# The input norm's weights as a column at the eviction of transposed chunks, dummy transposes ahead, and first gates in chains of 512 tokens

## The chip, the cores and the metric

The kernel runs on one core of one Trainium2 chip. Its time is in device microseconds (us), the median of several executions. Everything below names the core's engines as the profile does: PE (TensorE, matrix products; PEld is its weight loads), DVE (VectorE), ACT (ScalarE), POOL (GpSimd) and SP (SyncE, which here only issues transfers). SBUF is the on-chip memory, PSUM the eight banks of 128 x 512 floats into which PE writes.

## The reference

One layer of an encoder over 16 meta tokens and 1024 tokens of width 1024. The part that matters here is its beginning:

```python
def rms_norm(x, g):
    y = x * lax.rsqrt(jnp.mean(x * x, axis=-1, keepdims=True) + EPS)
    return y * g

a = rms_norm(h, norm_mix)                       # h: 16 meta tokens, then 1024 tokens
(q_na, k_na, v_na, q_hg, z_f, z_b, i_hg, g_hg, gate_na, gate_hg) = split_cols(a @ w_in)
log_f = logaddexp(log(lb), log1p(-lb) + log_sigmoid(z))      # per direction, from z_f and z_b
k = -expm1(log_f)                               # that is (1 - lb) * sigmoid(-z)
```

Here lb comes from a softmax over two rows of logits (`hg_lb_logits`). The rest of the layer (neighbourhood attention, a bidirectional gated recurrence over four heads, output projections, a feed-forward block, the final norm) follows and is not touched by the change.

## The kernel before

**Numbers and layout.** A product in full precision is made of three matmuls (`mm3`, lines 121 to 124): both operands are split into a rounded part `hi` and a remainder `lo`, and hi\*hi, hi\*lo and lo\*hi are accumulated in one PSUM bank. All projections contract over the 1024 features, in `KC` = 8 pieces of 128 (an index k), so one product of up to 512 tokens is 24 matmuls. The normed input must therefore lie with features on partitions: the tiles `aT[h]` hold it as hi and lo, `[128, 8, 512]` for each half h of 512 tokens, and the 16 meta tokens stand behind the first half, at columns 512 to 527.

**The beginning, function `start()`.** Tokens come as eight tiles `xt[i]` of 128 tokens x 1024 features, and the meta tokens as `xm` of 16 x 1024 (tile 8). For each tile:

- `square(i)`: ACT squares the tile with a running sum (line 554); POOL then works out 1/sqrt(mean + eps) in two operations on one column (lines 92 and 93);
- `scale(i)`: DVE multiplies the tile by that column and by the norm's weights in one scalar_tensor_tensor (line 559). The weights are needed along the free axis on all partitions, so a row of 1024 weights is spread over the partitions first, by two products with a column of ones (line 542) and two copies by ACT (line 545);
- `transpose(i)`: eight transposes on PE into two banks, each bank holding four feature pieces of 128 tokens (line 567);
- `evict(i)`: ACT copies a bank as hi, DVE takes the remainder as lo (lines 575 and 576).

Between the tiles stand the splits of the first two weight blocks (`load_block`, lines 112 and 113: hi by ACT, lo by DVE) and parts of the first products. `first_products` (a generator, one step per k) makes the gates' projections of head 0: forward (d = 0) and backward (d = 1), each for the two halves of the tokens. The forward one for the first half is made in two pieces, the first 256 tokens early, then 256 tokens and the 16 meta tokens in one piece of 272 columns. `start()` makes the first piece and the backward product of the first half; `rest()` makes the others. At the end of `start()` comes the small softmax for lb (tiles `lt`, `mx`; lines 631 to 642). The meta tokens are the last tile.

**The gates.** `gates_of` takes the finished products in the order in which they stand in `firsts`. For each, ACT makes two Sigmoids from PSUM (lines 220 and 221) and DVE three tensor_scalar operations (lines 222 and 225); for the meta tokens the same on 16 columns (lines 229 to 232). Its tiles (`T0`, `X0`, `Y`, ...) come from the pool `hp`, which is opened after `start()` has closed its own pool.

**What sets the order.** `start()`, `rest()` and the first part of head 0 stand in a block whose order is written out by hand: every engine issues its instructions in the order of the program's text. What follows the block is ordered by a planner that works with estimated times. SP issues the loads of tiles and weights, in the order x0, x1, forward weights, x2, x3, x4, backward weights, x5, x6, x7; ACT issues the weights of the norm, the meta tokens, the logits `lt` and a gain. Weight blocks pass through two `raw` buffers (line 102), so the third block's load waits until the first is split. PSUM at this stage: two banks for `mm`, two for `mx`, four for `a`.

## Time and profile before

| | |
|---|---|
| time, median of 3 runs | 1534.61 us (1534.53 to 1535.69) |
| the profiled execution: span | 1534.6 us |
| PE busy | 1503.2 us (98%) |
| DVE, ACT, POOL busy | 1031.3, 658.9, 380.1 us |
| granted TensorE clock, mean | 0.999 |
| HBM read, written | 139.56 MB, 54.53 MB |

The page of a profile gives the busy time of each engine, the span in 40 slices, the transfers by queue, the chain of work that ended last, and the costliest groups of instructions. A group's row reads: line, engine, operation, what is written from what, shapes, count | busy us, mean ns of one | idle time of the engine ahead of them and what ended it. A row of the timeline reads: start, duration (of several merged instructions with their count x2, x8: of all of them), engine, line, operation, and in brackets the idle time of the engine ahead of it. A row of the windows reads: the stretch, its length, the busy time of PE, PEld, DVE, ACT and POOL with counts, then the granted clock, the share of the DMA engines and GB/s. A row of the transfers ends in the KB of one and the us from its issue to its landing.

### The profile page before, as it was taken

The numbers are of one execution on the slowest core, as the hardware profiler recorded it, in microseconds if no ns is written. First come the engines' busy times: TensorE is split into PE (matmuls) and PEld (weight loads), VectorE is DVE, ScalarE is ACT, GpSimd is POOL, SyncE is SP. The second block draws the span as 40 slices with busy tenths as digits, with TensorE's granted clock in tenths as the row PEclk, the third lists the DMA queues.
The fourth block names the chain that finished last, engine by engine and source line by source line (L and its number), as shares of the span: only waits on it lengthen the run. The fifth ranks groups of instructions, "written<-read, shape, count | busy, mean of one in ns | idle before, by whom it ended". The sixth has DMA issues, their size and how long they took to land.

```text
span 1534.6 us, 23451 instructions
## 1 busy us (share of the span) xinstructions
PE 1503.2 (98%) x9192; PEld 1252.2 (82%) x9192; DVE 1031.3 (67%) x1603; ACT 658.9 (43%) x1175; POOL 380.1 (25%) x354
## 2 busy tenths in 40 slices
PE   7999999999999998999999999999999999999998
PEld 5888888878888887888888887888888888888886
DVE  6676666654876877666476358877777544877876
ACT  6231313125665666434123135555555533434444
POOL 2323131316315400011000122533333300231142
PEclk9999999999999999999999999999999999999999
DMA  4111111114123128434746123444444676563224
GB/s 167 45 29 56 29 56 29 56 29 130 56 66 120 62 65 272 138 124 153 261 163 233 42 97 117 165 154 153 153 153 150 208 266 236 193 232 111 96 83 151
DMA packets 142449, 195.61 MB, mean 127 GB/s; under 512 B 8049, under 2 KB 90097, under 8 KB 142338
## 3 DMA queue, kind: packets, MB, share of 16 engines
q1 hardware_dynamic: 133216, 172.53, 33.9%
q10 hardware_dynamic: 6946, 14.24, 2.4%
q0 software_dynamic: 2176, 7.34, 1.3%
q8 instruction: 72, 1.18, 0.3%
q14 instruction: 39, 0.32, 0.1%
HBM read 139.56 MB, written 54.53 MB: 126 GB/s over the span
## 4 chain that ended last, share of the span: by engine, by line
PE 89%; DVE 5%; issue 2%; ACT 2%; DMA 1%; POOL 1%; ACTq 0%; POOLq 0%; SPq 0%; DVEq 0%
PE mm L122 11%; PE mm L123 11%; PE mm L124 11%; PE mm L1349 5%; PE pa L1349 4%; PE pb L856 4%; PE pb L858 4%; PE pb L857 4%; PE pc L1349 4%; PE pb L1349 4%; PE pc L858 3%; PE pc L857 3%; PE pc L856 3%; PE pa L858 2%; PE pa L857 2%
## 5 line engine op out<-in xcount | busy, mean ns | idle before, releaser
L122 PE MATMUL mm<-aT,hi 128*128 128x512 f32 (+2 forms) x640 | 229.8, 359 | 2.4 <-DVE QX L727 1.5
L124 PE MATMUL mm<-aT,lo 128*128 128x512 f32 (+2 forms) x640 | 226.9, 354 | 0.5 <-DVE lo L113 0.5
L123 PE MATMUL mm<-aT,hi 128*128 128x512 f32 (+2 forms) x640 | 225.8, 353 | 0.0
L122 PEld LDWEIGHTS mm<-aT,hi 128*128 128x128 f32 x640 | 121.4, 190 | 16.6 <-issue 1.7
L124 PEld LDWEIGHTS mm<-aT,lo 128*128 128x128 f32 x640 | 121.3, 190 | 14.2 <-DVE lo L113 1.0
L123 PEld LDWEIGHTS mm<-aT,hi 128*128 128x128 f32 x640 | 121.4, 190 | 12.5
L97 DVE TENSOR_TENSOR dl<-ur,dh 128x1024 fp32r<-128x1024 f32 x54 | 71.0, 1315 | 87.3 <-ACT dh L96 87.1
L96 ACT CAST dh<-ur 128x1024 fp32r<-128x1024 f32 x54 | 56.9, 1054 | 166.5 <-issue 91.1
L112 ACT CAST hi<-raw 128x1024 fp32r<-128x1024 f32 x36 | 37.8, 1050 | 96.7 <-PE mm L123 68.4
L1154 DVE TENSOR_TENSOR wl<-raw,wh 128x512 fp32r<-128x512 f32 x50 | 40.9, 822 | 36.5 <-ACT wh L1153 36.3
L1158 ACT ACTIVATE uv<-uv 128x512 f32<-128x512 f32 x48 | 30.4, 633 | 80.0 <-DVE uv L1266 48.9
L1154 DVE TENSOR_TENSOR wl<-sx,wh 128x512 fp32r<-128x512 f32 x70 | 61.0, 882 | 3.4 <-ACT wh L1153 3.3
L1153 ACT CAST wh<-sx 128x512 fp32r<-128x512 f32 x70 | 42.3, 620 | 42.3 <-PE pc L857 24.0
L1439 POOL TENSOR_TENSOR w<-w,tt 128x512 f32<-128x512 f32 x16 | 23.4, 1460 | 132.9 <-DVE tt L1438 113.2
L300 POOL TENSOR_TENSOR Y<-X,TN 128x512 f32<-128x512 f32 x20 | 34.3, 1713 | 84.5 <-DVE X L297 84.5
L113 DVE TENSOR_TENSOR lo<-raw,hi 128x1024 fp32r<-128x1024 f32 x36 | 46.8, 1300 | 9.8 <-ACT hi L112 9.7
L782 DVE CUSTOM_DVE_ANT_0 pr<-nsc,NB 128x432 f32<-128x432 f32 (+1 forms) x64 | 35.2, 560 | 26.7 <-PE nsc L777 26.5
L409 DVE TENSOR_TENSOR QQ<-QQ,TN 128x512 f32<-128x512 f32 x48 | 35.1, 742 | 22.9 <-PE sc L404 22.9
L856 PE MATMUL pb<-nt,wh 128*128 128x512 f32 x128 | 50.2, 392 | 0.3 <-DVE uv L1236 0.2
L122 PE MATMUL mm<-wh,mT 128*128 128x512 f32 x128 | 50.1, 392 | 0.0
L858 PE MATMUL pb<-nt,wl 128*128 128x512 f32 x128 | 49.8, 389 | 0.0
L124 PE MATMUL mm<-wh,mT 128*128 128x512 f32 x128 | 49.8, 389 | 0.0
(391 smaller groups left out, 4370.9 us busy)
## 6 DMA issues: line engine op xcount, KB each, us to landing
raw<-in_w_in SPq DMA_DIRECT2D x56, 512.0 KB, 4.0
ur<-usp SPq DMA_DIRECT2D x54, 512.0 KB, 3.4
raw<-in_w_up SPq DMA_DIRECT2D x16, 1024.0 KB, 6.1
usp<-us SPq DMA_DIRECT2D x60, 256.0 KB, 2.2
sg<-gsp SPq DMA_DIRECT2D x16, 512.0 KB, 3.3
w<-in_w_dn SPq DMA_DIRECT2D x16, 512.0 KB, 4.5
usp<-uv SPq DMA_DIRECT2D x30, 256.0 KB, 3.2
gsp<-gv ACTq DMA_DIRECT2D x24, 256.0 KB, 2.4
```

The source lines that it names most:

```text
L96: act.copy(hi, src)
L97: dve.tensor_tensor(lo, src, hi.bitcast(F32), op=ALU.subtract)
L113: dve.tensor_tensor(lo[:, :kc], raw[:, :kc], hi[:, :kc].bitcast(F32), op=ALU.subtract)
L122: pe.matmul(ps, lh, rh, start=first, stop=False)
L123: pe.matmul(ps, lh, rl, start=False, stop=False)
L124: pe.matmul(ps, ll, rh, start=False, stop=last)
L856: pe.matmul(ps, lhs[0][:, c], rhs[0][:, k], start=first and k == 0, stop=False, skip_group_check=True)
L857: pe.matmul(ps, lhs[0][:, c], rhs[1][:, k], start=False, stop=False, skip_group_check=True)
L858: pe.matmul(ps, lhs[1][:, c], rhs[0][:, k], start=False, stop=k == 3, skip_group_check=True)
L1153: act.copy(v(hi), src)
L1154: dve.tensor_tensor(v(lo), src, v(hi).bitcast(F32), op=ALU.subtract)
L1349: pe.matmul(ps, a[n == 2][:, q, j * P:(j + 1) * P], b[n == 1][:, q], start=first and n == 0, stop=last and n == 2, skip_group_check=True)
```

## The change

The norm's weights no longer multiply the tiles ahead of the transposes. They come as a tile `g_col` of 128 x 8, feature on partition (the host passes the vector reshaped), and multiply when a transposed bank is evicted, since there the features lie on partitions. The banks hold now one feature piece k of all 512 tokens of a half (`turn`, `chunk`), and one eviction makes hi by an ACT multiply and lo by a DVE scalar_tensor_tensor. Tiles are scaled in place by their column alone. The meta tokens come first, with the softmax's first steps; they take their weights in one DVE product over 16 columns a piece.

PE gets transposes of the identity into a bank that nobody reads (`keep_warm`): 20 at the start, 8 after the meta tokens and 5 after each of tiles 0 to 2. Transposes of pieces 0 to 5 of the first half follow tile by tile; pieces 6 and 7 and the second half go piece by piece.

The forward product of the first half is one chain over 512 tokens, and the 16 meta tokens are a product of their own. The first gate is taken within `start()`, ahead of the scales of tiles 6 and 7. For this the gates' tiles come from a pool `hq` that is opened ahead of `start()`.

Work moves between engines: the split of the forward weights takes half of its lo to POOL, and the backward weights are split by POOL alone; the squares of tiles 6 and 7 go from ACT to DVE. Loads go in the order x0 to x3, forward weights, backward weights, x4 to x7; ACT's queue starts with the meta tokens, then `g_col`.

```diff
-                ev(ps[:, :n], t0, n)
+                if n:
+                    ev(ps[:, :n], t0, n)
...
+    def first_products(d, h, tag, n=TH):
+
+        nm = NM if n == NM else 0
+        c0 = TH if nm else 0
+        ps = bank(tag, "mm").rearrange("p a b -> p (a b)")[:, :n]
...
+        act.dma_start(xt[8], meta)
+        act.dma_start(g_col, g_mix)
...
+        for i in range(4):
             load_x(i)
+        raws = [load_raw(w_in[:, c:c + P], KC) for c in (C_ZF, C_ZB)]
+        for i in range(4, 8):
             load_x(i)
...
+            if eng is act:
+                act.activation(junk[:n], t, AF.Square, accum_out=sums[i][:n])
+            else:
+                dve.tensor_tensor_reduce(out=junk[:n], in0=t, in1=t, scale=1.0, scalar=0.0,
+                                         op0=ALU.mult, op1=ALU.add, accum_out=sums[i][:n])
...
         def scale(i):
+            dve.tensor_scalar(xt[i], xt[i], rs[i][:xt[i].shape[0]], None, op0=ALU.mult)
...
+        def keep_warm(n):
+            for j in range(n):
+                pe.transpose(warm[:, j % 4], ident, ident)
+
+        def turn(i, ks):
+            for k in ks:
+                pe.transpose(pts[i // 4, k][:, i % 4], xt[i][:, k * P:(k + 1) * P], ident)
+
+        def chunk(h, k):
+            pts[h, k] = bank("a", "pt")
+            for i in range(4 * h, 4 * h + 4):
+                turn(i, (k,))
+
+        def evict(h, k):
+            hi, lo = (t[:, k, :TH] for t in aT[h])
+            pt = pts[h, k].rearrange("p a b -> p (a b)")
+            act.mul(hi, pt, g_col[:, k:k + 1])
+            dve.scalar_tensor_tensor(lo, pt, g_col[:, k:k + 1], hi.bitcast(F32), op0=ALU.mult, op1=ALU.subtract)
...
+        def block(d):
+            hi, lo = blocks[d] = [wp.tile([P, KC, P], F32R, tag=t, name=t) for t in ("hi", "lo")]
+            copy, first = (pool.tensor_copy, pool) if d else (act.copy, dve)
+            copy(hi, raws[d])
+            for e, c in (first, slice(0, 4)), (pool, slice(4, 8)):
+                e.tensor_tensor(lo[:, c], raws[d][:, c], hi[:, c].bitcast(F32), op=ALU.subtract)
+
+        keep_warm(20)
         square(8)
+        root(8)
         scale(8)
+        ptm = bank("mm", "ptm")[:, 0].rearrange("p (k t) -> p k t", t=NM)
+        for k in range(KC):
+            pe.transpose(ptm[:, k], xt[8][:, k * P:(k + 1) * P], ident[:NM, :NM])
+        keep_warm(8)
         dve.tensor_tensor(mx, lt[:, :, 0], lt[:, :, 1], op=ALU.max)
+        for q in range(2):
+            pool.tensor_tensor(lt[:, :, q], lt[:, :, q], mx, op=ALU.subtract)
+        for k in range(6):
+            pts[0, k] = bank("a" if k < 4 else "mx", "pt")
+        for i in range(4):
+            square(i)
+            root(i)
+            scale(i)
+            turn(i, range(6))
+            if i < 3:
+                keep_warm(5)
+            if i == 0:
+                mh, ml = (t[:, :, TH:TH + NM] for t in aT[0])
+                dve.tensor_tensor(am, ptm, fap(g_col, 0, [[1, KC], [0, NM]]), op=ALU.mult)
+                act.copy(mh, am)
+                dve.tensor_tensor(ml, am, mh.bitcast(F32), op=ALU.subtract)
+                act.activation(lt.rearrange("p a b c -> p (a b c)"), lt.rearrange("p a b c -> p (a b c)"), AF.Exp)
+            if i == 1:
+                pool.tensor_tensor(mx, lt[:, :, 0], lt[:, :, 1], op=ALU.add)
+            if i == 2:
+                dve.reciprocal(mx, mx)
+        block(0)
...
+        f0 = first_products(0, 0, "mm")
+        evict(0, 0)
+        evict(0, 1)
+        for k in range(6):
+            some(f0, 1)
+            if k < 2:
+                chunk(0, k + 6)
+            evict(0, k + 2)
+            if k == 2:
+                square(4)
+        block(1)
+        some(f0, 2)
+        square(5)
+        root(4)
+        root(5)
+        for i in (6, 7):
+            square(i, dve)
+            root(i)
+        scale(4)
+        scale(5)
+        b0 = first_products(1, 0, "mm")
+        next(gates)
+        scale(6)
+        scale(7)
+        some(b0, 6)
+        f1 = first_products(0, 1, "mx")
+        for k in range(KC):
+            chunk(1, k)
+            evict(1, k)
+            if k < 2:
+                some(b0, 1)
+            if k > 2:
+                some(f1, 1)
         p0s.close()
+        return f1
+
+    def rest(gates, f1):
+
+        list(f1)
         next(gates)
         next(gates)
+        list(first_products(0, 0, "mm", NM))
+        next(gates)
+        early[C_Q] = block_of(C_Q)
+        list(first_products(1, 1, "mx"))
+        next(gates)
...
+        hq = hps.enter_context(tc.tile_pool(name="hq", bufs=1, reuse_waits="tile"))
...
+        f1 = start(ahead[0])
+        hp = hps.enter_context(tc.tile_pool(name="hp", bufs=1, reuse_waits="tile"))
+        rest(ahead[0], f1)
```

## The prediction

> **What bounds the kernel now.** I read the page first, then the early stretches window by window, then the first 60 us as a timeline by engine, then the groups with shapes kept apart for the price of each new operation.

> ```profile
> span 1534.6 us, 23451 instructions
> ...
> PE 1503.2 (98%) x9192; PEld 1252.2 (82%) x9192; DVE 1031.3 (67%) x1603; ACT 658.9 (43%) x1175; POOL 380.1 (25%) x354
> ```

> ```profile
> 0.00:10.00 10.00, 4.42 (x7) 1.83 (x8) 1.29 (x2) 5.21 (x8) 2.65 (x12) 1.00 0.85 290
> 10.00:20.00 10.00, 7.80 (x37) 7.03 (x36) 9.67 (x11) 7.87 (x15) 4.52 (x7) 1.00 0.81 295
> 20.00:30.00 10.00, 9.03 (x55) 7.35 (x54) 7.18 (x10) 7.34 (x14) 2.57 (x8) 1.00 0.18 52
> 30.00:40.00 10.00, 10.00 (x55) 7.99 (x53) 7.33 (x17) 5.54 (x12) 1.46 (x6) 1.00 0.01 2
> ```

> The first number after the stretch is its length, then the busy time of PE, PE's weight loads, DVE, ACT and POOL. PE idles 31.4 us in all, and 8.75 of them lie in the first 30 us, the part that the change rewrites; from 30 us on PE is full. So whatever the rewritten part gains or loses moves the rest as a whole, and it is enough to predict when the last of the first products ends. Before, that is where the next projection's first matmul starts, 48.70:

> ```profile
> 9.33 3.97 PE L567 MATMUL pt<-ident,na 128*128 128x128 f32 x16 [2.27 <-DVE na L559]
> ...
> 19.76 1.91 PE L567 MATMUL pt<-ident,na 128*128 128x128 f32 x8
> ...
> 22.95 1.04 PE L567 MATMUL pt<-ident,na 128*128 128x128 f32 x8
> ...
> 34.06 0.66 PE L567 MATMUL pt<-ident,na 16*128 16x16 f32 x8
> ```

> ```profile
> 40.23 0.28 PE L122 MATMUL mm<-aT,hi 128*128 128x272 f32 x1
> ...
> 43.23 0.39 PE L122 MATMUL mm<-aT,hi 128*128 128x512 f32 x1
> ...
> 48.70 0.39 PE L122 MATMUL mm<-aT,hi 128*128 128x512 f32 x1
> ```

> Prices on PE: 24 matmuls of 512 columns take 43.23 to 48.70, 5.47 us (0.68 per k of three); 24 of 272 columns take 3.00 (0.125 each). Eight transposes take 1.91 at 19.76 but 1.04 at 22.95: PE runs at about half pace until some 21 us, although the granted clock reads 1.00. Warm, a transpose is 0.13.

> **The change, part by part.** (1) *The matmul count.* The first forward product ran as 256 and 272 columns, at most 3.00 each when warm; now it runs as 512 (5.47) and 16. The 16-column matmul with a full weight load is not in the trace. Its bounds are 0.075 (the 16x16 transposes, 8 in 0.66 with their tail) and 0.125 (272 columns): 1.8 to 3.0 for 24. I take 2.4, between them, as the load of full weights is common to it and the 272-column row. Together 7.9, at least 1.9 more than 6.0; against that, part of the 256 columns ran ahead of the rise in pace.

> (2) *The dummy transposes* are 43 in all, 20 before anything else. The first 20 cost at most 20 x 0.24 = 4.8 us from 1.5 us on, ahead of any data. Those between the tiles stand in waits for DVE: zero, as long as the scale of the next tile ends later than they do.

> (3) *The start of the chain.* Meta tokens and the lower-bound softmax come first now, and they stand ahead of tile 0 on three engines: on DVE the max over lt, on POOL the two subtractions ahead of tile 0's root, on ACT the meta copy and the Exp ahead of tile 1's square.

> ```profile
> xt<-in_x SPq DMA_DIRECT2D x8, 512.0 KB, 7.2
> ...
> xm<-in_meta ACTq DMA_DIRECT2D x1, 64.0 KB, 4.7
> ...
> lt<-in_lbl ACTq DMA_DIRECT2D x1, 8.0 KB, 7.0
> ```

> ```profile
> 1.65 0.43 ACTq L529 DMA_DIRECT2D lt<-in_lbl  x1
> ...
> 2.10 3.07 SPq L522 DMA_DIRECT2D xt<-in_x  x3
> ...
> 5.87 1.06 ACT L554 ACTIVATE na<-xt 128x1024 f32<-128x1024 f32 x1
> ...
> 7.10 0.58 ACT L545 COPY g_bc<-pg 128x512 f32<-128x512 f32 x1
> 7.11 0.19 POOL L92 TENSOR_SCALAR rtm<-ssq 128x1 f32<-128x1 f32 x1 [5.68 <-ACT na L554]
> ...
> 7.99 1.28 DVE L559 SCALAR_TENSOR_TENSOR na<-xt,rs,g_bc 128x1024 f32<-128x1024 f32 x1 [7.99 <-POOL rs L93]
> ...
> 33.82 0.15 DVE L631 TENSOR_TENSOR mx<-lt 128x8 f32<-128x8 f32 x1
> ...
> 34.05 0.20 POOL L632 TENSOR_TENSOR lt<-lt,mx 128x8 f32<-128x8 f32 x1 [3.52 <-DVE mx L631]
> ```

> On SP's queue tiles 2 and 3 now go ahead of both weight blocks: fourth, as at 2.10 before, tile 3 lands near 2.10 + 7.2 = 9.3, ahead of its square. The weights, fifth and sixth now, are wanted only from 15.5 on, and tiles 4 to 7 after 24; the next weight block's load, which waits for a raw buffer, is wanted after 46. No load sets the path. lt lands at 1.65 + 7.0 = 8.65. It stays third on ACT's queue, so I keep 8.65; bounds 6.0 (where xm landed) and 10.0. Then max 0.2, two subtractions 0.4, root to scale 0.88 (7.11 to 7.99): tile 0's scale starts at about 10.2, where it was 7.99. The Exp on 16 columns, the meta product on DVE and its copy on ACT then add about 0.85 (four times the Exp's 0.21) before tile 1's square, which starts near 11.8.

> ```profile
> 34.44 0.21 ACT L637 ACTIVATE lt<-lt 128x16 f32<-128x16 f32 x1 [1.04 <-POOL lt L633]
> ```

> (4) *The scale.* It loses its tensor operand (the weights), so it becomes a one-source operation. The nearest row is L786, in place with one column scalar.

> ```profile
> L786 DVE TENSOR_SCALAR pr<-pr,rc x64: 360/437/1057, 381.8 to 577.1; 128x432 f32<-128x432 f32 x48, 128x288 f32<-128x288 f32 x16
> ```

> From 288 columns (0.36) to 432 (0.437) is 0.53 ns a column, so 1024 cost 0.75 against 1.28. [...] If a scale cost 1.08 (one column per 1.04 ns), the sum below would be 1.3 worse.

> Squares on ACT follow each other every 1.23 (5.87, then the next operation at 7.10). Tile 3's square ends at 11.8 + 3 x 1.23 = 15.5; root to scale 0.88, and 0.3 for one root waiting behind a scale, so its scale runs 16.7 to 17.45.

> (5) *The weights at the eviction.* ACT's copy from PSUM becomes a multiply with a column; the nearest row is the copy that it replaces, 0.59, less than DVE's part and so hidden behind it. DVE's lo becomes a SCALAR_TENSOR_TENSOR from PSUM:

> ```profile
> L575 ACT CAST aT<-pt 128x512 fp32r<-128x512 f32 x16 | 8.9, 588 | 6.1 <-PE pt L567 6.1
> ```

> ```profile
> L782 DVE CUSTOM_DVE_ANT_0 pr<-nsc,NB 128x432 f32<-128x432 f32 x48 | 28.4, 596 | 0.0
> ...
> L492 DVE SCALAR_TENSOR_TENSOR ot<-opt,gain_sb,gs 128x512 f32<-128x512 f32 x8 | 5.7, 748 | 6.1 <-PE opt L490 6.1
> ...
> L97 DVE TENSOR_TENSOR lo<-raw,hi 128x512 fp32r<-128x512 f32 x8 | 5.5, 683 | 0.0
> ...
> L782 DVE DVE_READ_ACCUMULATOR2_ANT mn<- 128x1 f32 x64 | 5.3, 83 | 0.0
> ```

> ```profile
> 15.23 1.28 DVE L576 TENSOR_TENSOR aT<-pt,aT 128x512 fp32r<-128x512 f32 x2
> ...
> 18.82 1.27 DVE L559 SCALAR_TENSOR_TENSOR na<-xt,rs,g_bc 128x1024 f32<-128x1024 f32 x1
> ```

> In a row such operations overlap by 0.08 (two of 0.68 in 1.28), so 0.67 each, 5.4 for eight. DVE first does its half of the forward weight block (0.68), and it can meet POOL there:

> ```profile
> 16.01 0.19 POOL L92 TENSOR_SCALAR rtm<-ssq 128x1 f32<-128x1 f32 x1 [0.28 <-ACT na L554]
> ...
> 19.16 0.99 POOL L92 TENSOR_SCALAR rtm<-ssq 128x1 f32<-128x1 f32 x1 [2.33 <-ACT na L554]
> ...
> 46.45 1.30 POOL L286 TENSOR_TENSOR kd<-X,Y 128x512 f32<-128x512 f32 x1
> 50.72 2.23 POOL L286 TENSOR_TENSOR kd<-X,Y 128x512 f32<-128x512 f32 x1 [2.96 <-DVE X L225]
> ```

> The 0.19 operation at 19.16 takes 0.99, to 20.15, until DVE's ends at 20.09; the second kd takes 2.23 for the first one's 1.30. So POOL and a DVE operation with two SBUF inputs shut each other out. [...] I charge half of one POOL operation, 0.65 (bounds 0 and 1.3). The last lo of the first half then ends at 17.45 + 0.68 + 0.65 + 5.4 = 24.2.

> (6) *Tiles 4 to 7.* DVE now squares tiles 6 and 7. L782 is the nearest reduce: 432 columns in 0.596, so 1024 in 1.21 at 1.04 ns a column, plus 0.08 to read the sum: 2.6 for two. Then four scales at 0.67, and in the middle the first gate:

> ```profile
> 41.06 0.55 DVE L222 TENSOR_SCALAR T<-sf,oml_sb,lb_sb 128x512 f32<-128x512 f32 x1 [2.48 <-ACT sf L220]
> ...
> 41.82 0.35 DVE L225 TENSOR_SCALAR Y<-sn,oml_sb 128x256 f32<-128x256 f32 x1
> ```

> 1.1 us. The Sigmoids ahead of it and their table load on ACT are hidden: ACT ends its last square near 24, and DVE reaches the gate at about 28.7. With 0.5 for the roots behind POOL's second block (bounds 0 and 2.4), tile 7's scale ends at 24.2 + 2.6 + 0.5 + 2.7 + 1.1 = 31.1. PE meanwhile does the first forward product from about 19.5 (8 x 0.68 and two chunks of four transposes, 1.0) to 26.0 and six k of the backward one to 30.1; so it idles one microsecond, and up to that the half pace would cost nothing.

> (7) *The rest on PE*, after 31.1, without a gap: 0.13, then seven chunks at 0.5 (3.5), two k (1.36), 5.47, meta 2.4, 5.47: 18.3, so 49.4. The chunks' evictions (0.67) fit into their 1.18 of PE time. The query block's split, on ACT and DVE, lies under the last 5.47, as before.

> **Sum:** 49.4 against 48.70, 0.7 later. The profiled execution's 1534.6 equals the median of 1534.61, so 1535.3. The early wins (no broadcast of the weights, whole-bank evictions, cheaper scales) are given back by the later first scale and by DVE's queue ahead of tile 7.

> **The rivals.** *POOL becomes the bound (slower).* POOL gets a copy of 1024 columns (not in the trace; 1.3 to 2.6 by kd) and three halves at 1.3 or more. From about 19.2 that ends at 23.1 at best and 25.2 at worst. Beyond 24.2 the squares of tiles 6 and 7 and the four roots take turns with it, each scale then comes a root and a scale (0.75 + 0.67 = 1.4) after the one before, and tile 7 is ready at 33.5: 2.4 later, and 0.65 from (5). 1534.6 + 0.7 + 3.05 = 1538.4. For it: kd's 2.23. Against: the lo evictions have one operand in PSUM, and POOL's operation at 16.01 kept its 0.19 beside such a pair (15.23 to 16.51).

> *All goes well.* lt lands with xm (0.9 earlier), no lock (0.65 and 0.5), 16 columns at 0.075 (0.6), though PE's own chain then binds: from a first product at 18.0 us it needs 28.7 (four times 5.47, 1.8, and ten chunks at 0.5), ending at 46.7: 2.0 earlier, 1532.6, still within 0.2%.

> *The dummies don't raise the pace.* Before, PE transposed for 3.97 us from 9.33 on and was still slow at 19.76. If the gaps while PE waits for scales keep it slow through the first half of the first product's 6.4 us, that half takes 3.2 longer, less the 1.0 of slack: 2.2, so 1534.6 + 0.7 + 2.2 = 1537.5. [...]

> *The later order changes.* Only the beginning has its order written out; the rest is planned from estimated times, and a shifted beginning can reorder it. A tenth of PE's 31.4 us idle time either way is 3.1 us: 1531.4 or 1537.8.

> **How the numbers follow.** A measurement of this kernel tells about 0.2% (3.07 us) from no change: below 1531.5 is faster, above 1537.7 slower. Forecast 0.47 (own range 1534 to 1537), POOL 0.18, all well 0.15, half pace 0.08, reordering 0.12. Faster: half of the reordering and 0.07 for errors common to all terms, 0.13. Slower: most of POOL 0.14, half of the half pace 0.04, half of the reordering 0.06, 0.24. Same 0.63. The range runs from 1532 (all well, with the best of the bounds) to 1539.5 (POOL with part of the half pace).

> **What would show it.** Tile 0's scale starting near 10.2 and waiting on POOL; scales of 0.75; DVE unbroken from tile 3's scale to tile 7's; a PE gap of about 1 us before tile 7's transposes; the query projection near 49.4. Wrong if lt lands before 7, if POOL's second block ends after 24.2, if transposes at 17 us still take 0.24, or if the path from the query projection to the end is not 1485.9.

## The result, and the profile after

The changed kernel takes 1539.82 us, median of six executions (1536.91 to 1541.67), against 1534.98 for the kernel before on the same chip (1534.53 to 1536.17). The ratio is 1.0031, with a 95% interval of 1.002 to 1.0043: slower by 3 to 6.6 us, where 0.7 was forecast, and above the upper end of the range, 1539.5. The same kernel run again gave 1539.00, just inside that range, and 1.0028 (1.0018 to 1.0039).

The page of the changed kernel's profile, its first rows, and then its windows (columns as in the prediction: length; PE, PEld, DVE, ACT, POOL busy; granted clock; share of the DMA engines; GB/s):

```profile
span 1536.4 us, 23516 instructions
...
PE 1509.1 (98%) x9231; PEld 1260.5 (82%) x9231; DVE 1030.0 (67%) x1603; ACT 656.6 (43%) x1165; POOL 385.7 (25%) x357
```

```profile
0.00:10.00 10.00, 6.22 (x36) 5.55 (x36) 1.04 (x3) 3.47 (x5) 2.59 (x13) 1.00 0.87 284
10.00:20.00 10.00, 8.54 (x39) 8.05 (x39) 5.08 (x9) 5.19 (x11) 7.10 (x12) 0.50 0.66 253
20.00:30.00 10.00, 9.77 (x47) 7.90 (x46) 9.38 (x15) 8.46 (x14) 6.53 (x8) 0.99 0.36 102
30.00:40.00 10.00, 8.76 (x52) 7.06 (x51) 6.68 (x11) 4.43 (x7) 2.11 (x3) 1.00 0.00 0
```

PE looks busier than before in the first 20 us, but these are the dummies. The granted clock reads 0.50 from 10 to 20, in spite of them. Its record has 1.00 from 6.50 to 9.91, 0.50 from there to 20.15, and then 1.00 again: the changes lie 3.41 and three times 3.41 us apart. Stretches of this length are meant where the clock's windows or stretches are spoken of below. DVE, 9.67 busy from 10 to 20 before, is down to 5.08 there and up from 7.18 to 9.38 from 20 to 30: part of its work comes a window later. From 30 to 40, where PE was full, it now lacks 1.24.

How the loss stands in time: every operation of DVE and ACT was matched with the same operation of the kernel before, from 50 us on. The later order is the same on every engine. After minus before is +2.8 at 50 us and +3.0 at 300, +1.5 at 650, +1.9 from 1000 to the end. Against a second execution of the kernel before it is +3.6, +3.8, +2.6 and +3.1. So the loss is there before the query projection starts. Behind it, 1.4 is made good between 515 and 545: PE of both executions of the kernel before waits there twice for DVE (near 521 and 540), and of neither of the changed one. The same program, too, gains or loses one or two microseconds from execution to execution. That gives the yardstick for the experiments: the start of the last gate's Sigmoid, which ends the first products (0.2 behind the query projection's first matmul). In the kernel before, twice; then in the changed kernel, twice (the timeline of ACT of four executions):

```profile
48.90 0.60 ACT L220 ACTIVATE sf<-mm 128x512 f32<-128x512 f32 x1 [3.73 <-PE mm L124]
```

```profile
48.03 0.60 ACT L220 ACTIVATE sf<-mm 128x512 f32<-128x512 f32 x1 [3.73 <-PE mm L124]
```

```profile
51.67 0.60 ACT L220 ACTIVATE sf<-mm 128x512 f32<-128x512 f32 x1 [4.41 <-PE mm L124]
```

```profile
52.66 0.60 ACT L220 ACTIVATE sf<-mm 128x512 f32<-128x512 f32 x1 [5.78 <-PE mm L124]
```

48.0 to 48.9 has become 51.7 to 52.7, 2.8 to 4.6 later; the medians are 4.1 to 4.8 apart. How it came about is read from DVE, POOL and PE of the changed kernel, in three timelines. DVE:

```profile
9.87 0.75 DVE L553 TENSOR_SCALAR xt<-xt,rs 128x1024 f32<-128x1024 f32 x1 [1.41 <-POOL rs L93]
...
14.73 0.75 DVE L553 TENSOR_SCALAR xt<-xt,rs 128x1024 f32<-128x1024 f32 x1 [0.72 <-POOL rs L93]
...
16.20 1.75 DVE L553 TENSOR_SCALAR xt<-xt,rs 128x1024 f32<-128x1024 f32 x1 [0.61 <-POOL rs L93]
17.87 0.68 DVE L585 TENSOR_TENSOR lo<-raw,hi 128x512 fp32r<-128x512 f32 x1
20.00 3.39 DVE L574 SCALAR_TENSOR_TENSOR aT<-pt,g_col,aT 128x512 fp32r<-128x512 f32 x5 [1.44 <-ACT aT L573]
23.93 2.07 DVE L574 SCALAR_TENSOR_TENSOR aT<-pt,g_col,aT 128x512 fp32r<-128x512 f32 x3 [0.55 <-ACT aT L573]
...
32.31 0.75 DVE L553 TENSOR_SCALAR xt<-xt,rs 128x1024 f32<-128x1024 f32 x1 [0.72 <-POOL rs L93]
```

POOL, the forward block's half and the backward block:

```profile
16.13 1.27 POOL L585 TENSOR_TENSOR lo<-raw,hi 128x512 fp32r<-128x512 f32 x1
...
18.57 1.03 POOL L583 CAST hi<-raw 128x1024 fp32r<-128x1024 f32 x1
19.68 2.53 POOL L585 TENSOR_TENSOR lo<-raw,hi 128x512 fp32r<-128x512 f32 x2
```

PE:

```profile
15.40 1.27 PE L559 MATMUL warm<-ident 128*128 128x128 f32 x5
16.47 1.49 PE L563 MATMUL pt<-ident,xt 128*128 128x128 f32 x6
17.75 1.27 PE L559 MATMUL warm<-ident 128*128 128x128 f32 x5
18.82 1.48 PE L563 MATMUL pt<-ident,xt 128*128 128x128 f32 x6
...
33.12 0.33 PE L563 MATMUL pt<-ident,xt 128*128 128x128 f32 x1 [1.14 <-DVE xt L553]
...
43.29 0.17 PE L122 MATMUL mm<-aT,hi 128*128 128x16 f32 x1
...
45.88 0.49 PE L122 MATMUL mm<-aT,hi 128*128 128x512 f32 x1
...
51.47 0.39 PE L122 MATMUL mm<-aT,hi 128*128 128x512 f32 x1
```

Tile 2's scale is done at 15.48, but its transposes start at 16.47: they queue behind five dummies at half pace. Tile 3's scale takes 1.75 instead of 0.75, beside POOL's half block (16.13 to 17.40), and its transposes again start behind dummies. So DVE stands still for 1.44, and the first lo is at 20.00. Tile 7's scale ends at 33.06, behind a wait of 0.72 for its root, and PE stands for 1.14. The row of 24 matmuls of 16 columns takes 2.59.

### The profile page after: what moved, and what is told of

The parts are those of the page before. It is cut to its first block, busy times and chain, and to the rows that moved or that the text cites. A ratio compares the mean times of both kernels' runs of the same rounds, so it can differ in the third digit from the quotient of the medians.

```text
span 1536.4 us, 23516 instructions
## 1 busy us (share of the span) xinstructions
PE 1509.1 (98%) x9231; PEld 1260.5 (82%) x9231; DVE 1030.0 (67%) x1603; ACT 656.6 (43%) x1165; POOL 385.7 (25%) x357
## 3 DMA queue, kind: packets, MB, share of 16 engines
q0 software_dynamic: 2176, 7.34, 1.3%
q8 instruction: 72, 1.18, 0.3%
## 4 chain that ended last, share of the span: by engine, by line
PE 90%; DVE 4%; issue 2%; ACT 2%; DMA 1%; POOL 1%; ACTq 0%; POOLq 0%; DVEq 0%
PE mm L122 11%; PE mm L123 11%; PE mm L124 11%; PE mm L1361 5%; PE pa L1361 4%; PE pb L868 4%; PE pb L870 4%; PE pb L869 4%; PE pb L1361 4%; PE pc L1361 4%; PE pc L870 3%; PE pc L868 3%; PE pc L869 3%; PE pa L868 2%; PE pa L870 2%
## 5 line engine op out<-in xcount | busy, mean ns | idle before, releaser
L122 PE MATMUL mm<-aT,hi 128*128 128x512 f32 (+2 forms) x640 | 230.0, 359 | 1.6 <-DVE QX L739 1.5
L122 PEld LDWEIGHTS mm<-aT,hi 128*128 128x128 f32 x640 | 120.9, 189 | 15.6 <-issue 1.7
L97 DVE TENSOR_TENSOR dl<-ur,dh 128x1024 fp32r<-128x1024 f32 x54 | 71.1, 1316 | 87.3 <-ACT dh L96 85.3
L1170 ACT ACTIVATE uv<-uv 128x512 f32<-128x512 f32 x48 | 30.4, 633 | 80.0 <-DVE uv L1278 48.9
L1451 POOL TENSOR_TENSOR w<-w,tt 128x512 f32<-128x512 f32 x16 | 23.4, 1462 | 132.9 <-DVE tt L1450 116.9
L868 PE MATMUL pb<-nt,wh 128*128 128x512 f32 x128 | 50.2, 392 | 0.3 <-DVE uv L1248 0.2
L122 PE MATMUL mm<-wh,mT 128*128 128x512 f32 x128 | 50.2, 392 | 0.0
L869 PE MATMUL pb<-nt,wh 128*128 128x512 f32 x128 | 49.9, 389 | 0.0
## 6 DMA issues: line engine op xcount, KB each, us to landing
raw<-in_w_in SPq DMA_DIRECT2D x56, 512.0 KB, 4.0
ur<-usp SPq DMA_DIRECT2D x54, 512.0 KB, 3.6
sg<-gsp SPq DMA_DIRECT2D x16, 512.0 KB, 4.1
w<-in_w_dn SPq DMA_DIRECT2D x16, 512.0 KB, 5.0
```

Of the source, the lines that this page charges most:

```text
L97: dve.tensor_tensor(lo, src, hi.bitcast(F32), op=ALU.subtract)
L122: pe.matmul(ps, lh, rh, start=first, stop=False)
L868: pe.matmul(ps, lhs[0][:, c], rhs[0][:, k], start=first and k == 0, stop=False, skip_group_check=True)
L869: pe.matmul(ps, lhs[0][:, c], rhs[1][:, k], start=False, stop=False, skip_group_check=True)
```

## The experiments

In all of them the milestone is the last gate's Sigmoid, as above. The ratios are against the kernel before on the same chip. The runs with medians come from three chips, on which the kernel before took 1534.88, 1534.92 and 1535.03, so the medians can be set side by side.

| run | what it is | median | ratio (95%) | milestone |
|---|---|---|---|---|
| b_again | before | 1535.21 | 1.0001 (0.9992 to 1.001) | 48.03 |
| a_again | changed | 1539.00 | 1.0028 (1.0018 to 1.0039) | 52.66 |
| a_nodummy | changed, no dummies | 1538.22 | 1.0019 (1.001 to 1.0029) | 50.99 |
| a_hot | changed, more dummies | 1538.08 | 1.0017 (1.0008 to 1.0027) | 52.01 |
| a_metamix | changed, small row spread | 1537.30 | 1.0018 (1.0009 to 1.0028) | 50.47 |
| a_lock | changed, forward lo all on DVE | 1538.57 | 1.0029 (1.0017 to 1.004) | 50.43 |
| a_late | changed, softmax and meta later | 1536.76 | 1.0015 (1.0006 to 1.0025) | 48.33 |
| b_meta16 | before, with the small row | 1537.32 | 1.0016 (1.0007 to 1.0025) | 49.58 |
| c_comb | last three edits of "changed" together | 1534.82 | 1.0000 (0.9992 to 1.0009) | 49.59 |
| c_all | c_comb and more of the kind | 1533.07 | 0.9991 (0.9982 to 1.0) | 44.35 |
| c_all_nod | c_all without dummies | 1531.69 | 0.9978 (0.9969 to 0.9987) | 46.23 |

**The two kernels again.** No edit; they give the spread that a single trace has.

> The kernel before, once more, for its spans, its clock and a second profile. If the spread of the changed kernel (1536.9 to 1541.7) comes from where the clock's windows fall in the beginning, the kernel before should spread less (1534.5 to 1536.2 so far), its first transposes should again run at half pace (0.24 each), and the rise of the pace should lie at another time than 21.5 us. If the spread is the chip's, both spread alike. Each time should stand about 1.8 us above its span, as in the changed kernel.

> The changed kernel, once more. Clock theory: another execution falls on other windows, so the pace at tiles 0 to 3 (half from 9.9 to 20.2 us in the first profile) differs, and the query projection starts elsewhere than at 51.5 us, by up to 2 us; the time stays 3 to 6 us above the kernel before. Rival (a fixed loss in the order of work): the projection starts again within 0.3 us of 51.5.

The kernel before repeats within 0.01%; its ten times spread over 4.4 us, those of the changed one over 6.7. The changed one repeats its loss, and its second trace holds what the first does not show. The windows of that second trace, three stretches next to each other:

```profile
41.75:45.10 3.35, 3.35 (x29) 3.15 (x27) 2.14 (x6) 1.17 (x3) 1.30 (x1) 1.00 0.02 5
45.15:48.50 3.35, 3.35 (x10) 2.77 (x10) 1.66 (x3) 1.19 (x3) 2.00 (x6) 0.50 0.01 2
48.55:52.00 3.45, 3.45 (x16) 2.82 (x15) 0.00 (x0) 0.00 (x0) 0.28 (x2) 1.00 0.61 176
```

and its PE there:

```profile
42.73 0.17 PE L122 MATMUL mm<-aT,hi 128*128 128x16 f32 x1
...
45.51 0.77 PE L122 MATMUL mm<-aT,hi 128*128 128x512 f32 x1
46.08 0.63 PE L123 MATMUL mm<-aT,hi 128*128 128x512 f32 x1
46.51 0.63 PE L124 MATMUL mm<-aT,lo 128*128 128x512 f32 x1
...
48.84 0.39 PE L124 MATMUL mm<-aT,lo 128*128 128x512 f32 x1
```

The row of 16-column matmuls (42.73 to 45.51) takes up 2.41 of one stretch, 41.72 to 45.13, in which PE is busy throughout by the record; in the next the clock is halved, and the 512-column matmuls follow every 0.43 instead of 0.23. The 24 of them behind the row take 6.96 instead of 5.59, 1.4 more. In the first trace the row lies 43.29 to 45.88, with at most 1.84 of it in one stretch, and the clock stays at 1.00. In every trace here the changes of the clock lie 3.41 us or a multiple of it apart, and at other times in each execution. Counted so, seven traces hold the row in one piece: the clock falls behind it in the two in which 2.41 (a_again) and 2.60 (a_hot) of it lie in one stretch, and in none of the five in which it is 2.00 or less. In both of these the record shows PE busy throughout the stretch ahead of the fall (3.35 of 3.35 us read in a_again, 3.30 of 3.30 in a_hot).

**The dummies taken away, and made enough to fill the gaps.**

```diff
-        keep_warm(20)
...
-        keep_warm(8)
...
-            if i < 3:
-                keep_warm(5)
```

```diff
-        keep_warm(20)
+        keep_warm(25)
...
-        keep_warm(8)
+        keep_warm(24)
...
-                keep_warm(5)
+                keep_warm((18, 5, 4)[i])
```

> The changed kernel without any dummy transposes. If the dummies at half pace are what holds up tile 3's transposes (they started at 18.8, 0.9 after the tile's scale ended), these start right behind the scale, but the first product then runs at half pace until a whole busy stretch has passed, near 24 us: the query projection at 51 to 53, the time within 1.5 us of the changed kernel's on either side. Rival (the dummies are only a cost): about 1 us faster than the changed kernel, no product at half pace for longer.

> The changed kernel with 25 dummies at the start, 24 after the meta tokens and 18, 5 and 4 after tiles 0, 1 and 2, so that PE has no idle stretch before the first product. If the half pace from 9.9 to 20.2 us delays tile 3, its transposes now end near 18.8 instead of 20.3, the first product starts 1.0 to 1.3 earlier and the whole gets 1 us faster than the changed kernel, with less spread. If DVE and POOL alone set the path (the scale of tile 3 and the roots), no change within 0.3 us.

The transposes without dummies, and with more of them (timelines of PE):

```profile
18.24 1.54 PE L557 MATMUL pt<-ident,xt 128*128 128x128 f32 x6 [0.91 <-DVE xt L553]
...
19.49 0.80 PE L122 MATMUL mm<-aT,hi 128*128 128x512 f32 x1
```

```profile
17.67 0.88 PE L563 MATMUL pt<-ident,xt 128*128 128x128 f32 x6 [0.88 <-DVE xt L553]
...
18.78 0.51 PE L122 MATMUL mm<-aT,hi 128*128 128x512 f32 x1 [0.23 <-ACT aT L573]
```

Without any, the pace is half until 23.4 (four transposes take 0.71 at 21.30 and 0.36 at 23.43), and PE has then been busy without a gap since 18.24. Enough dummies do hold the clock (0.88 for six transposes against 1.54), and the first product starts 0.7 earlier than without any (18.78 against 19.49). In the changed kernel, with the dummies as given, it starts at 20.02, later than in both. Yet both versions end 0.8 to 0.9 below the changed kernel, with intervals that overlap its own. The dummies as given gain nothing that can be measured; the clock that they raise falls again in the gaps between them (full 6.5 to 9.9 in the changed kernel's trace, then half to 20.15). Nor do they always raise it: of the ten traces below and above with the first 20 dummies as given, the clock rises at 4.2 to 6.5 in eight, but only at 16.9 in a_metamix and 13.7 in c_comb. In these two no stretch of 3.41 holds more than 2.6 of the 20; in the other eight one holds 2.8 or more. In a_hot the row of 16 columns fell wholly into one stretch, and the clock halved behind it from 45.17 to 48.59, as in a_again.

**The row of 16 columns spread between other work.** Its 24 matmuls go, three at a time, between the transposes and 512-column products of the second half; nothing is left out.

```diff
         f1 = first_products(0, 1, "mx")
+        fm0 = first_products(0, 0, "mm", NM)
...
             if k > 2:
                 some(f1, 1)
+                some(fm0, 1)
...
-        list(first_products(0, 0, "mm", NM))
```

> The changed kernel with the 24 matmuls of 16 columns interleaved, three by three, with the second half's forward product, instead of standing in a row. In two profiles the granted clock halved for one stretch of 3.41 us right behind that row (45.13 to 48.54), in a third it did not (the row straddled two stretches). If the row of small matmuls causes the fall, it is gone: no half clock between 25 and 60 us, the query projection 0 to 1.7 us earlier (1.0 on the mean), the time 1 us faster than the changed kernel. If the fall has another cause (the microsecond of idle before tile 7), it stays and the time too.

```profile
35.00:48.00 13.00, 13.00 (x79) 11.38 (x78) 8.00 (x16) 6.85 (x13) 2.49 (x3) 1.00 0.01 2
```

The window of this trace holds all 24 of them, and the clock stays full. They are hardly shorter here (from one chunk's transposes to the next PE takes 1.44 with three of them and 1.14 without), so what can be saved is the fall. In none of the eight traces of this page with the row spread (here, c_comb and those behind it) does the clock fall at the row or behind it up to 60 us. The median is 1.7 below a_again; the intervals of the two overlap.

**The small row in the kernel before.** Its piece of 272 columns is cut into 256 and 16, and the gates take one step more for it.

```diff
-        for d, q in ((0, (0, 1, 0, TH, TH, 0)), (0, (0, 0, 256, 256, 256, NM)), (1, (1, 1, 0, TH, TH, 0))):
+        for d, q in ((0, (0, 1, 0, TH, TH, 0)), (0, (0, 0, 256, 256, 256, 0)), (0, (0, 0, TH, 0, 0, NM)), (1, (1, 1, 0, TH, TH, 0))):
```

> The kernel before with one part of the change alone: its last forward piece of 272 columns made as 256 and, by itself, 16 columns. By the matmuls alone 24 x 0.111 = 2.7 us more, less 0.1: 2.6 slower. If a row of small matmuls also halves the clock behind it in most executions, 3 to 4.3 slower, and a half-clock stretch near 45 us in the profile. If small matmuls were free behind the larger ones, no change.

It makes the kernel before slower by 0.16%, about 2.4 us, with nothing else of the change in it; the profiled execution shows no fall of the clock behind the row (41.21 to 43.81), and its milestone is 0.7 to 1.6 later. By length, 24 of 256 columns (0.12 each) and 24 of 16 (0.111) take 2.5 more than 24 of 272 (0.125), so the row's length alone would move the median as far; the clock is known of one execution only. In the change itself this 2.6 is part of step 1.

**POOL's half block.** The forward block's lo wholly on DVE.

```diff
-            for e, c in (first, slice(0, 4)), (pool, slice(4, 8)):
+            for e, c in (first, slice(0, 4)), (first, slice(4, 8)):
```

> The changed kernel with the whole lo of the forward weights on DVE, so that POOL has no 1.27 us operation in the way of tile 3's scale (it took 1.75 for 0.75). If POOL and DVE shut each other out, that scale takes 0.75 again and the first product starts up to 1.0 earlier, less what PE's dummies at half pace take back (0.9 at most) and 0.6 more DVE work: 0 to 0.5 us faster. If the 1.75 has another cause, it stays, and the time rises by 0.6.

```profile
16.07 0.75 DVE L553 TENSOR_SCALAR xt<-xt,rs 128x1024 f32<-128x1024 f32 x1 [0.60 <-POOL rs L93]
16.73 2.13 DVE L585 TENSOR_TENSOR lo<-raw,hi 128x512 fp32r<-128x512 f32 x2
18.79 3.37 DVE L574 SCALAR_TENSOR_TENSOR aT<-pt,g_col,aT 128x512 fp32r<-128x512 f32 x5
```

Tile 3's scale is back at 0.75, so its 1.0 was POOL's doing. But now DVE's own two halves take 2.13 instead of some 1.3, beside POOL, which has turned to the backward block and takes 1.49 for its copy at 16.83 instead of 1.03: each takes longer beside the other. The first lo starts 1.2 earlier, in an execution whose clock was full again from 16.75, not 20.15, so not all of it need come from POOL. The median moves by 0.4, which is less than the interval tells.

**Softmax and meta tokens behind tile 3.** The max and the subtractions, the Exp, the sums and the meta product move from the front of the chain to behind the first half's evictions.

```diff
-        dve.tensor_tensor(mx, lt[:, :, 0], lt[:, :, 1], op=ALU.max)
-        for q in range(2):
-            pool.tensor_tensor(lt[:, :, q], lt[:, :, q], mx, op=ALU.subtract)
...
         block(0)
+        dve.tensor_tensor(mx, lt[:, :, 0], lt[:, :, 1], op=ALU.max)
+        for q in range(2):
+            pool.tensor_tensor(lt[:, :, q], lt[:, :, q], mx, op=ALU.subtract)
...
             evict(0, k + 2)
+            if k == 0:
+                act.activation(lt.rearrange("p a b c -> p (a b c)"), lt.rearrange("p a b c -> p (a b c)"), AF.Exp)
...
+            if k == 1:
+                dve.reciprocal(mx, mx)
...
+            if k == 3:
+                mh, ml = (t[:, :, TH:TH + NM] for t in aT[0])
+                dve.tensor_tensor(am, ptm, fap(g_col, 0, [[1, KC], [0, NM]]), op=ALU.mult)
```

> The changed kernel with the softmax for lb and the meta tokens' product with the weights moved behind tile 3; the meta tokens' square, scale and transposes stay first. If these small steps in front hold up the tiles, tile 0's scale starts near 7.2 instead of 9.9 and tile 3's near 12 instead of 16.2, the first product near 15 instead of 20; the query projection then comes 3 to 5 us earlier and the kernel is as fast as before or up to 2 us faster. Rival (the loads bind: tiles and weights land too late): at most 1 us.

```profile
12.07 1.75 DVE L553 TENSOR_SCALAR xt<-xt,rs 128x1024 f32<-128x1024 f32 x1 [0.72 <-POOL rs L93]
...
14.97 2.73 DVE L574 SCALAR_TENSOR_TENSOR aT<-pt,g_col,aT 128x512 fp32r<-128x512 f32 x4 [0.47 <-ACT aT L573]
...
28.98 0.75 DVE L553 TENSOR_SCALAR xt<-xt,rs 128x1024 f32<-128x1024 f32 x1 [0.71 <-POOL rs L93]
```

The first lo starts at 14.97, 5.0 earlier, yet tile 7's scale only 3.3 earlier, at 28.98: there DVE's squares and the roots that take turns with the scales set the pace. The milestone goes with tile 7, 48.33, and the median falls by 2.2. It stays 1.8 above the kernel before, where level or better was expected, although the milestone is level with that kernel's.

**The three together, and a version mended further.** c_comb is a_late, a_metamix and a_lock in one. c_all also gives POOL the backward block right behind the forward one, and has all squares on ACT, each with its root at once; the max and the subtractions go ahead of tile 3's scale, the reciprocal and the meta product behind the squares (here against c_comb):

```diff
         block(0)
...
+        block(1)
...
             if k == 1:
...
+                square(4)
+                root(4)
             if k == 3:
...
+                square(5)
+                root(5)
...
         for i in (6, 7):
-            square(i, dve)
+            square(i)
             root(i)
```

c_all_nod is c_all without the dummies.

> The three edits of a_late, a_metamix and a_lock together in the changed kernel. Theory 1: the loss of the change lies wholly ahead of the query projection, and its parts add. Alone the three moved the median by -2.2 (1536.8 against 1539.0), -1.7 (1537.3) and -0.4 (1538.6); together -4.3: about 1534.7, ratio 0.9998 to the kernel before, its query projection near 46.5 to 47.5. Theory 2: something that does not hang on the beginning costs about 1.5 us in the changed kernel (a_late began the query projection at 48.3 like the kernel before, and still took 1.8 more): then about 1536.2, ratio 1.001, though the query projection starts before 47.5.

> c_comb, and more of the same kind: the second weight block on POOL right behind the first (POOL was idle 13 to 18 in a_late), squares 4 to 7 all on ACT and each with its root at once (no square on DVE), the meta product's rows and the softmax's reciprocal behind the first half's evictions. Theory 1: first product near 14.5, tile 7's scale ended by 25 (29.7 in a_late), so no gap on PE ahead of the second half's transposes; query projection near 45.2, 3.3 earlier than in the kernel before: 1531 to 1532, ratio 0.998. Theory 2: the same start, 1533 to 1533.5, ratio 0.999.

> c_all without the dummy transposes (it computes the same). If they are worth what they were put there for: tile 3's transposes and the first products at half clock up to a full stretch, first product about 0.8 later and the first two or three steps 0.5 longer each, query projection 1 to 2 later and the time 1 to 2 more than c_all. If they are worth nothing (in the changed kernel it was 0.8 faster without them): within 0.5 of c_all.

c_comb's median is level with the kernel before, and its interval is clear of a_again's: the three edits together undo the loss. The sum of the single edits said so (1534.7 forecast, 1534.82 measured), closer than it could know, since each of them is known to about 1.5 us only. Where the loss is undone is not shown. Theory 1 put it all ahead of the query projection and its start at 46.5 to 47.5; the trace has its milestone at 49.59, 0.7 to 1.6 behind the kernel before (its clock was full only from 13.7), and it draws level later, as PE lacks the two waits near 521 and 540. c_all comes out 0.09% ahead, at the edge of its interval. Its milestone is even earlier than forecast (44.35 against 45.2), yet 1533.07 is the time of theory 2, so part of what the beginning gains is lost behind it. c_all_nod wins clearly, 0.22% or 3.3 us, and beats both kernels. Its DVE has tile 7 ready before PE asks for it (timeline of c_all_nod):

```profile
12.08 0.75 DVE L553 TENSOR_SCALAR xt<-xt,rs 128x1024 f32<-128x1024 f32 x1 [0.64 <-POOL rs L93]
...
24.53 0.75 DVE L553 TENSOR_SCALAR xt<-xt,rs 128x1024 f32<-128x1024 f32 x1 [0.71 <-POOL rs L93]
```

and PE runs from 15.60 to the milestone with no wait in it. In its trace the operations stand 2.7 ahead of the first execution of the kernel before at 50 us and 2.85 at the end (1.8 and 1.7 against the second).

**Why without dummies is not slower.** In the traces of c_all and c_all_nod the milestone is 1.9 earlier with dummies, while the median is 1.4 later. The times of c_all lay in two groups, so three more traces of it were taken, and one more of the version without.

> c_all once more, for its trace. Its eleven times fall into two groups, 1531.8 to 1533.1 and 1534.3 to 1535.9; the profiled one (1532.9) is of the lower. Theory 1: in an execution of the upper group the clock, which the dummy transposes raise early, has fallen again by the time of the first products (full first, then half up to 13 or later), the first products run at half pace and the query projection begins near 46.5 instead of 44.35. Theory 2: the beginning is the same (query projection 44.2 to 44.6) and the 2 us lie later, in a fall of the clock behind 45. An execution of the lower group shows 44.2 to 44.6 and the full clock from 5 or 6 on by either.

> The same kernel and the same question as c_all_2: above 1534, a query projection near 46.5 (theory 1) or near 44.4 (theory 2).

> The same kernel and the same question as c_all_2: above 1534, a query projection near 46.5 (theory 1) or near 44.4 (theory 2).

> c_all without the dummies once more, for its trace: its ten times lie between 1530.9 and 1533.5, the profiled one (1533.5) at the top with its query projection at 46.23. A usual execution (1531.7): by theory 1, which puts all differences into the beginning, the query projection begins near 44.5; by theory 2, which puts them later, near 46.2.

| run | time | milestone | clock in the beginning |
|---|---|---|---|
| c_all | 1532.88 | 44.35 | full from 5.5 |
| c_all_2 | 1533.45 | 46.26 | full 5.9 to 16.2, half to 19.6 |
| c_all_3 | 1533.00 | 45.29 | full 4.4 to 7.8, half to 11.2 |
| c_all_4 | 1535.76 | 46.18 | full 5.5 to 15.8, half to 19.2 |
| c_all_nod | 1533.51 | 46.23 | full 12.7 to 16.1, half to 19.5 |
| c_all_nod_2 | 1533.32 | 46.21 | full 12.3 to 15.7, half to 19.1 |

Neither theory holds as it was put. The dummies raise the clock at 4 to 6 in all four traces, but in two of them it falls at 16 all the same, as it does without dummies, after the stretch in which PE waits for the first evictions (1.11 us, to 15.59, in c_all_2); then the milestone is 46.2 with and without. That explains why they can be worth nothing. It does not explain c_all_4: with the beginning of c_all_2 it ends 2.3 later. Matched operation by operation, the two are level up to 220 us, and then c_all_4 falls back in steps, +0.9 at 221, +0.6 at 520, +0.8 at 537, +0.9 at 815, less 1.0 in between. The steps at 520 and 537 are waits for DVE that c_all_2 lacks. The first step, PE in c_all_2 and in c_all_4:

```profile
220.04 0.83 PE L405 MATMUL sc<-QQ,X 128*32 128x32 f32 x64 [0.62 <-DVE QQ L410]
```

```profile
220.01 0.64 PE L405 MATMUL sc<-QQ,X 128*32 128x32 f32 x51 [0.62 <-DVE QQ L410]
221.42 0.32 PE L405 MATMUL sc<-QQ,X 128*32 128x32 f32 x13 [0.78 <-issue]
```

In the middle of a row of 64 matmuls PE stands for 0.78 us and waits for nothing that the profile shows. At 818 it waits 0.6 for an operand whose weights were split 2.9 us later than in the other execution, behind their load. These come and go between executions of one program.

One difference does go with the dummies in these six traces. In all four of c_all PE waits twice for DVE near 461 and 480, as here in c_all_2; in neither of the two without does it:

```profile
462.84 0.41 PE L809 MATMUL ppt<-ident,pr 128*128 128x128 f32 x2 [0.42 <-DVE pr L798]
...
481.63 0.47 PE L122 MATMUL mm<-aT,hi 128*128 128x512 f32 x1 [0.63 <-DVE KL L748]
```

Matched between 455 and 500 us, the four lose 1.3 to 1.6 there on the two, about the 1.4 between the medians. The same pair of waits near 519 and 537 stands in five of the six (not in c_all_2). What brings these waits about, and whether the dummies do, stays open; the intervals of the two medians overlap slightly.

## Why the prediction was wrong

The forecast was no change, 1535.3; it is 0.3% slower. The sum put the query projection at 49.4; it started at 51.47 in the profiled execution, 2.1 later, and at 52.47 in the second. By its steps:

- **(1) The count of matmuls.** Forecast 2.4 for the 24 of 16 columns, measured 2.59; the bounds held. What failed is the step's silence on the clock: it priced the row by its own length, and in a_again and a_hot the clock was 0.50 for the 3.41 us behind the row, 1.4 more in a_again. Nothing in the prediction had this.
- **(2) The dummies.** "Zero, as long as the scale of the next tile ends later than they do." The condition failed for tiles 2 and 3: at half pace five take 1.27, and the transposes started 1.0 and 0.9 behind their scales. The prediction's own sign of being wrong, a transpose of 0.24 at 17 us, is there (six in 1.49 at 16.47). Without dummies the first product starts 0.5 earlier, with the clock held full 1.2 earlier. This is the step that fell most clearly, and the condition that it leant on was left unchecked against the 0.24 that the same text had read for a slow transpose: six transposes and five dummies at 0.24 make 2.6, more than the 1.47 between two scales.
- **(3) The start of the chain** was right: lt's max started at 8.29 where 8.65 was assumed, tile 0's scale at 9.87 against 10.2. The wait behind lt that it priced was real; a_late, which takes it and the meta product out of the way, has the first lo 5.0 earlier. That delay stood in the forecast, so it is part of the loss against the kernel before (a_late's median is 2.2 lower) and not of the miss.
- **(4) The scale** was right at 0.75.
- **(5) The evictions.** 0.67 each held (five in 3.39). That POOL and DVE hold each other up (the prediction's "lock") was met, as 1.0 on tile 3's scale (1.75 for 0.75) and not as 0.65 on the weights' lo (0.68). "DVE unbroken" was wrong: it waited 1.44 for ACT, which waited for PE's late transposes, and 0.55 more where ACT put square 4 between two evictions. ACT's part was called hidden, which is true of one eviction and not of the row. The last lo of the first half ended at 26.00, not 24.2, and this 1.8 is nearly all of the 2.1.
- **(6) Tiles 4 to 7.** The pieces held: two squares in 2.4 (2.6 forecast, at 1.04 ns a column; in the kernel before, line 97's `lo<-raw,hi` took 0.683 with 512 columns and 1.222 with 1024, 1.05 ns a column), the gate 1.1, one wait of 0.72 on a root (0.5), PE's gap 1.14 (one microsecond). Tile 7's scale ended at 33.06 against 31.1, late by what (5) had handed on.
- **(7) The rest on PE** took 18.35 from 33.12 to 51.47; forecast 18.3.
- **The level.** "The profiled execution's 1534.6 equals the median" compared a span with a time. In every execution whose span and time both are known the time is 1.8 above the span (1536.41 and 1538.19 for the changed kernel), so the profiled execution of before took some 1536.4, 1.8 above its median. The sum added 0.7 to the right number by chance; but read from such an execution, the start at 48.70 was late for this kernel (a second trace has its milestone 0.9 earlier), and the difference may have been underestimated by as much.
- **What this accounts for.** The forecast difference was 0.7, the measured ones 4.1 and 4.8. The steps up to the query projection give 2.1, the level up to 0.9, the halved clock 1.4 in an execution that has it. The profiled execution, 1538.19, is 1.6 below its kernel's median, so how a median execution divides up is not shown.

Of the rivals, *POOL becomes the bound* gave 1538.4, nearest to the measured time, by a mechanism that was not met: POOL's second block ended at 22.2, before 24.2, since its copy took 1.03 where 1.3 to 2.6 was assumed. *The dummies don't raise the pace* (1537.5) was the nearest to what happened: the granted clock was 0.50 from 10 to 20. It had a chance of 0.08. In the stretch ahead of the fall (6.50 to 9.91) PE was busy for 1.69 of 3.41 us, and its longest gap was 2.03, 1.26 of it in that stretch. *The later order changes* is refuted, and so is *all goes well*.

## What to carry to other kernels

Filler instructions that stand ahead of other work on an engine are free only if they end before that work is ready, at the pace that the engine has if the filler fails; count them at the slow pace (here five took 1.27 at half pace and 0.71 at full, and tile 2's transposes started 1.0 late behind them). A row of very small matmuls can cost more than its length (in two of seven traces, 1.4 us in a_again), so mix it with large ones. And where PE is full afterwards, judge an edit of the beginning by when the last operand becomes ready (here tile 7's scale), since a first operand that is 5.0 earlier was worth 3.3 there and 2.2 in the median.
